# Second attention of a two-block network: heads side by side, and a fixed order of transposes, values and scores

## The chip, the core and the metric

The kernel runs on one core of a Trainium2 chip. The metric is device time in microseconds (us) for one execution of the whole program. Matrix products and transposes run on TensorE, reductions and copies on VectorE, exponentials and copies on ScalarE, element-wise work of the weights on GpSimd; SyncE issues most DMAs. Each engine works off its own instructions in the order in which the program holds them.

## What is computed

The program is a network of two blocks on a sequence of 1024 tokens of 1024 channels, in float32. The first block (gated linear attention, latent attention and an MLP, two layers) isn't touched. The second projects its input to the queries, keys and values of a dilated window attention with three groups (dilations 1, 4, 16) and eight heads of 64 channels, to the input of a Hyena convolution, and to gates. Of it the change concerns the window attention:

```python
DILATED_GROUPS = ((128, 1), (512, 4), (2048, 16))
...
    s = jnp.einsum('bdnqhe,bdnkhe->bdnhqk', qb, kw).astype(jnp.float32) * (E ** -0.5)
    s = s - slopes[:, None, None] * dist[:, None]
    s = jnp.where(valid[:, None], s, -jnp.inf)
    lse = jax.nn.logsumexp(s, axis=-1)
    p = jnp.exp(s - lse[..., None]).astype(v.dtype)
    o = jnp.einsum('bdnhqk,bdnkhe->bdnqhe', p, vw)
...
    wts = jax.nn.softmax(jnp.stack(lses, axis=0), axis=0)
    o_attn = jnp.einsum('gbsh,gbshe->bshe', wts.astype(x.dtype), jnp.stack(outs, axis=0))
```

Every query attends to the keys within a window of its group; the groups are then weighted by a softmax over their denominators.

## The kernel before

`block2` (L1540) first projects queries, keys and values, and then runs the attention in a loop over four pairs of heads (`hp`). In each turn `attention2` (L1681) loads the pair's queries, keys and values, turns the values (`vtp`, L1704) and goes through 16 steps of 128 queries: eight of part 0 (group 1, 256 keys), then eight of part 1 (groups 2 and 3 together, 256 + 128 keys). The two heads of a pair lie on partitions 0 to 63 and 64 to 127. A step is:

- **scores**: for each head one product of 256 keys (in part 1 another of 128) into a bank of its own, `as_ps` (tag "as", three buffers);
- **softmax**: for each head one VectorE operation that adds the distance bias and takes the maximum (L1737), then the negated maxima of both (`anb`, L1739), then for each head one exp on ScalarE with the sum beside it (L1741);
- **transposes**: two or three 128 x 128 blocks per head into `atp` (L1747, tag "sm", two buffers), copied to `apT` by VectorE for head 0 (L1751) and by ScalarE for head 1 (L1749);
- **values**: for each head two or three products with the values into `ao_ps` (tag "ao", one bank for four steps), copied out to `aoT` every fourth step (L1765).

A float32 product makes two records on TensorE, a transpose one. After the 16 steps `attention_weights` (L1769) weighs the two parts: the maxima and sums of part 1 go to a DRAM buffer (`abounce`, L1779) and come back in the order of part 0 (`anat`, L1780); small VectorE and ScalarE operations (L1784 to L1794) form the weights; two transposes turn them (`aw_tp`, L1798), products spread them over the heads (`aw_ps`), and VectorE and GpSimd combine the outputs.

Beside this the loop issues dense work: three column tiles of the Hyena projection per pair (`project_hyena`, L1637), each with 48 products of 512 columns (`in`, two halves of 24) and then eight transposes (`tp`, L1657) of the convolved tile `c3y`, which VectorE makes by two multiply-adds (L1208); in the last turn also gates. Their weights are split into a high and a low part by ScalarE (`w_hi`) and GpSimd or VectorE (`w_lo`, L214).

A scheduler sets the order of every engine's instructions from the order of the code, priorities, dependencies and the number of buffers of each tag. In the attention nothing else holds the order.

Of the kernel before, what the change touches and what calls it, by code (L numbers as in the profile page):

```python
# [9 lines left out]
F32 = mybir.dt.float32  # L10
# [3 lines left out]
AF = mybir.ActivationFunctionType  # L14
ALU = mybir.AluOpType
AX = mybir.AxisListType

S = 1024
# [143 lines left out]
class Kernel:  # L162
# [1474 lines left out]
    def project_hyena(self, cp, cw, ft, zd, xgd):  # L1637

        nc = self.nc
        c0 = 5120 + ft * 128  # L1640
        w = self.weights2(c0)
        u = cp.tile([128, S + 2], F32, name="c3u", tag="c3u", bufs=1)
        nc.gpsimd.memset(u[:, 0:1], 0.0)
        nc.gpsimd.memset(u[:, S + 1 : S + 2], 0.0)
        for hf in range(2):
            ps = self.project2(c0, w, hf)
            with self.tc.high_priority():
                nc.scalar.activation(u[:, 1 + hf * 512 : 513 + hf * 512], ps, AF.Identity, bias=self.bias2(c0))
        y = cp.tile([128, S], F32, name="c3y", tag="c3y", bufs=1)
        nc.scalar.activation(y, u[:, 1 : S + 1], AF.Identity, scale=cw[:, ft, 1:2], bias=cw[:, ft, 3:4])  # L1650
        self.fma(y, u[:, 0:S], cw[:, ft, 0:1], y)
        self.fma(y, u[:, 2 : S + 2], cw[:, ft, 2:3], y)
        yield
        for b in range(2):
            tp = self.PS.tile([128, 4, 128], F32, name="tp2", tag="sm", bufs=2)
# [25 lines left out]
    def attention2(self, p, hp, qkvd, yad, dist, heads):  # L1681
        nc = self.nc
        scale = 0.125
        Q, K, V = [], [], []
        for g in range(3):
            w = 1152 if g == 0 else S
            o = 64 if g == 0 else 0
            q = p.tile([128, S], F32, name="aq", tag="aq", bufs=3)
            nc.sync.dma_start(q, qkvd[hp, g, 0])
            k = p.tile([128, 1152], F32, name="ak", tag="ak", bufs=3)  # L1690
            v = p.tile([128, 1152], F32, name="av", tag="av", bufs=1)
            if g == 0:
# [23 lines left out]
        outs = []  # L1716
        for part in range(2):
            oT = p.tile([128, S], F32, name="aoT", tag="aoT", bufs=2)
            n = 256 if part == 0 else 384
            nk = n // 128  # L1720
            for i in range(8):
                ps = [self.PS.tile([128, 512], F32, name="as_ps", tag="as", bufs=3) for h in range(2)]
                qc = slice(i * 128, i * 128 + 128)
                for h in range(2):
                    r = slice(64 * h, 64 * h + 64)
                    if part == 0:
                        self.mm(ps[h][:, 0:256], Q[0][r, qc], K[0][r, i * 128 : i * 128 + 256], True, True)
                    else:
                        c0 = (i // 2) * 256
                        self.mm(ps[h][:, 0:256], Q[1][r, qc], K[1][r, c0 : c0 + 256], True, True)  # L1730
                        self.mm(ps[h][:, 256:384], Q[2][r, qc], K[2][r, qc], True, True)
                b0 = (0 if i == 0 else 512 if i == 7 else 256) if part == 0 else 768 + 384 * (i % 2)
                s = p.tile([128, 2, 384], F32, name="as", tag="as", bufs=3)
                nb = p.tile([128, 2], F32, name="anb", tag="anb", bufs=4)
                at = i if part == 0 else (i % 2) * 4 + i // 2
                for h in range(2):
                    nc.vector.tensor_tensor_reduce(s[:, h, :n], ps[h][:, :n], bt[h][:, b0 : b0 + n], scale=1.0, scalar=-3.0e38,  # L1737
                                                   op0=ALU.add, op1=ALU.max, accum_out=mst[:, part, h, at : at + 1])
                nc.vector.tensor_scalar(nb, mst[:, part, :, at], -scale, None, op0=ALU.mult)  # L1739
                for h in range(2):  # L1740
                    nc.scalar.activation(s[:, h, :n], s[:, h, :n], AF.Exp, scale=scale, bias=nb[:, h : h + 1],  # L1741
                                         accum_out=sst[:, part, h, at : at + 1])
                pt = p.tile([128, 2, 3, 128], F32, name="apT", tag="apT", bufs=2)
                for h in range(2):
                    tp = self.PS.tile([128, 4, 128], F32, name="atp", tag="sm", bufs=2)
                    for k in range(nk):
                        nc.tensor.transpose(tp[:, k], s[:, h, k * 128 : k * 128 + 128], self.ident)  # L1747
                    if h:
                        nc.scalar.activation(pt[:, h, :nk], tp[:, :nk], AF.Copy)  # L1749
                    else:  # L1750
                        nc.vector.tensor_copy(pt[:, h, :nk], tp[:, :nk])  # L1751
                if i % 4 == 0:
                    ops = self.PS.tile([128, 4, 128], F32, name="ao_ps", tag="ao", bufs=1)
                for h in range(2):
                    hc = slice(64 * h, 64 * h + 64)
                    for k in range(nk):
                        if part == 0:
                            v = V[0][:, i + k, hc]
                        elif k < 2:
                            v = V[1][:, (i // 2) * 2 + k, hc]  # L1760
                        else:
                            v = V[2][:, i, hc]
                        self.mm(ops[hc, i % 4], v, pt[:, h, k], k == 0, k == nk - 1, tile_position=(0, 64 * h))
                if i % 4 == 3:
                    nc.vector.tensor_copy(oT[:, (i // 4) * 512 : (i // 4) * 512 + 512], ops.rearrange("p a b -> p (a b)"))  # L1765
            outs.append(oT)
        return self.attention_weights(p, outs, mst, sst, yad[hp], heads)

    def attention_weights(self, p, outs, mst, sst, dst, heads):  # L1769

        nc = self.nc
        scale = 0.125
        bounce = self.DR.tile([2, 2, S], F32, name="abounce", tag="abounce", bufs=2)
        nat = p.tile([128, 2, 2, 8], F32, name="anat", tag="anat", bufs=2)
        for n, t in enumerate((mst, sst)):
            for h in range(2):
                for m in range(2):
                    to = bounce[n, h].rearrange("(w b m a) -> m w b a", b=2, m=2, a=4)[m]
# [14 lines left out]
        for part in range(2):  # L1793
            nc.vector.tensor_mul(e[:, part], e[:, part], den[:, 0])  # L1794

        tp = self.PS.tile([128, 4, 128], F32, name="aw_tp", tag="sm", bufs=2)
# [6 lines left out]
        y = outs[0]  # L1803
        for part in range(2):
            for b in range(2):
                ps = self.PS.tile([128, 4, 128], F32, name="aw_ps", tag="sm", bufs=2)
                for a in range(4):
                    self.mm(ps[:, a], heads[:, 4 * b + a], et[:, part], True, True)
                c = slice(b * 512, b * 512 + 512)
# [2 lines left out]
                else:  # L1812
                    w = p.tile([128, 512], F32, name="awt", tag="awt", bufs=1)
# [191 lines left out]
```

## Time and profile before

| what | us |
|---|---|
| median of 3 runs | 4472.46 (4463.63 to 4475.19) |
| profiled execution | 4475.41 |
| its span, first to last instruction | 4473.6 |
| TensorE busy in the span | 4130.8 (92%) |
| VectorE busy | 2082.0 (47%) |
| ScalarE busy | 1488.5 (33%) |
| GpSimd busy | 1488.1 (33%) |
| mean granted TensorE clock | 0.963 |
| the attention of the second block | from about 3395 to 3812 |

The busy shares are means over the whole program. The attention's loop takes less than a tenth of the span, so what the change does to it is read from that stretch alone. A granted clock of 1.0 is the higher of TensorE's two levels (2.4 GHz), 0.5 the lower (1.2 GHz); a value between them is a mix of both in the stretch.

### The profile page before, as it was taken

What the parts mean: (1) busy time and instruction counts of PE and PEld (TensorE: products, weight loads), DVE (VectorE), ACT (ScalarE), POOL (GpSimd) and SP (SyncE); (2) the same over time, 40 slices, a digit from 0 to 9 for tenths busy, and PEclk for the clock granted to TensorE, in tenths of its full rate; (3) what the DMA queues carried; (4) which work ended last, traced back from release to release, by engine and by line L of the source; (5) the groups of instructions that cost most, each with busy time, mean ns of one, the idle gap of its engine ahead of it and who ended that gap; (6) DMA issues with size and microseconds to landing.
All of it is one profiled execution on the core that took longest, in us unless ns stands there. A gap on an engine that the chain in (4) does not pass through costs nothing. (4 is left out here: it accounts for less than half of the span.)

```text
span 4473.6 us, 53257 instructions
## 1 busy us (share of the span) xinstructions
PE 4130.8 (92%) x20132; PEld 3220.5 (72%) x20132; DVE 2082.0 (47%) x3791; ACT 1488.5 (33%) x2822; POOL 1488.1 (33%) x1349
## 2 busy tenths in 40 slices
PE   6999888999999899888999999899999999877998
PEld 4776666888886686676888887567777676766777
DVE  6336675332335516586233324642322443577546
ACT  5435444212123515445212121323224444222222
POOL 3322455333333412254433332131230111355342
PEclk8999899999999999899999999999999999998999
DMA  6245533221111135623211111344453321645563
GB/s 195 62 134 164 166 121 92 92 61 52 47 51 58 47 106 180 202 93 116 74 44 52 43 52 48 105 123 104 113 145 83 90 86 48 188 150 157 164 193 113
DMA packets 566388, 471.21 MB, mean 105 GB/s; under 512 B 197416, under 2 KB 460670, under 8 KB 566002
## 3 DMA queue, kind: packets, MB, share of 16 engines
q1 hardware_dynamic: 375514, 367.43, 27.0%
q10 hardware_dynamic: 189880, 92.63, 7.2%
q0 software_dynamic: 736, 7.73, 0.5%
q8 instruction: 159, 2.61, 0.2%
q14 instruction: 99, 0.81, 0.1%
HBM read 364.17 MB, written 107.47 MB: 105 GB/s over the span
## 5 line engine op out<-in xcount | busy, mean ns | idle before, releaser
L214 POOL TENSOR_TENSOR w_lo<-w_raw,w_hi 128x1024 fp32r<-128x1024 f32 (+4 forms) x222 | 411.0, 1852 | 1015.8 <-ACT w_hi L208 936.4
L205 PE MATMUL dn<-act,dn_hi 128*128 128x512 f32 x2048 | 636.5, 392 | 9.8 <-ACT act L208 4.2
L662 DVE SCALAR_TENSOR_TENSOR xa<-dn,mod,xa 128x512 f32<-128x512 f32 x512 | 383.9, 750 | 277.8 <-PE dn L205 276.0
L205 PE MATMUL in<-b2h,w_hi 128*128 128x512 f32 x1152 | 467.3, 406 | 5.5 <-ACT qkv_t L1626 5.5
L205 PE MATMUL in<-b2h,w_lo 128*128 128x512 f32 x1152 | 466.6, 405 | 0.0
L205 PE MATMUL in<-b2l,w_hi 128*128 128x512 f32 x1152 | 466.3, 405 | 0.0
L208 ACT ACTIVATE w_hi<-w_raw 128x1024 fp32r<-128x1024 f32 (+4 forms) x276 | 236.8, 859 | 683.1 <-PE in L205 249.2
L205 PEld LDWEIGHTS dn<-act,dn_hi 128*128 128x128 f32 x2048 | 386.1, 189 | 95.1 <-ACT act L208 5.3
L205 PE MATMUL up<-fh,w_hi 128*128 128x512 f32 x1024 | 405.9, 396 | 0.7 <-DVE relu L632 0.4
L205 PE MATMUL up<-fl,w_hi 128*128 128x512 f32 x1024 | 402.9, 393 | 1.9 <-POOL fl L214 1.5
L205 PE MATMUL up<-fh,w_lo 128*128 128x512 f32 x1024 | 404.0, 395 | 0.0
L205 PE MATMUL dn<-act,dn_lo 128*128 128x512 f32 x1024 | 401.0, 392 | 2.8 <-POOL dn_lo L214 2.8
L632 DVE TENSOR_TENSOR relu<-up,relu 128x512 f32<-128x512 f32 x128 | 88.4, 691 | 604.5 <-ACT relu L631 604.5
L214 POOL TENSOR_TENSOR dn_lo<-dn_raw,dn_hi 128x1024 fp32r<-128x1024 f32 x64 | 151.9, 2392 | 524.5 <-ACT dn_hi L208 524.5
L205 PEld LDWEIGHTS in<-b2h,w_hi 128*128 128x128 f32 x1152 | 225.4, 196 | 57.4 <-issue 8.5
L205 PEld LDWEIGHTS in<-b2h,w_lo 128*128 128x128 f32 x1152 | 225.2, 195 | 51.6 <-issue 7.3
L205 PEld LDWEIGHTS in<-b2l,w_hi 128*128 128x128 f32 x1152 | 225.1, 195 | 50.0 <-issue 6.2
L208 ACT ACTIVATE dn_hi<-dn_raw 128x1024 fp32r<-128x1024 f32 x64 | 64.7, 1052 | 553.4 <-PE dn L205 546.1
L214 POOL TENSOR_TENSOR act<-relu,act 128x512 fp32r<-128x512 f32 x128 | 167.7, 1311 | 190.4 <-ACT act L208 190.3
L205 PEld LDWEIGHTS up<-fl,w_hi 128*128 128x128 f32 x1024 | 192.5, 188 | 49.0 <-POOL fl L214 3.2
L205 PEld LDWEIGHTS up<-fh,w_hi 128*128 128x128 f32 x1024 | 192.4, 188 | 46.6 <-issue 1.4
L205 PEld LDWEIGHTS up<-fh,w_lo 128*128 128x128 f32 x1024 | 192.6, 188 | 45.5 <-issue 1.0
(502 smaller groups left out, 8349.0 us busy)
## 6 DMA issues: line engine op xcount, KB each, us to landing
wada<-in_w_ada SPq DMA_DIRECT2D x120, 512.0 KB
w_raw<-in_w_in SPq DMA_DIRECT2D x102, 512.0 KB
w_raw<-in_w_mlp_up SPq DMA_DIRECT2D x64, 512.0 KB
dn_raw<-in_w_mlp_down SPq DMA_DIRECT2D x64, 512.0 KB
qkv<-qkv_t ACTq DMA_DIRECT2D x72, 256.0 KB
w_raw<-in_w_out SPq DMA_DIRECT2D x64, 256.0 KB
mix<-mix SPq DMA_DIRECT2D x64, 256.0 KB
spectra<-spec ACTq DMA_DIRECT2D x32, 384.0 KB
```

Of the source, the lines that this page charges most:

```text
L205: return self.nc.tensor.matmul(out, lhsT, rhs, start=start, stop=stop, **kw)
L208: self.nc.scalar.activation(hi, x, AF.Copy, **kw)
L214: return eng.tensor_sub(lo, x, hi.bitcast(F32))
L632: nc.vector.tensor_mul(sq, ps, sq)
L662: nc.vector.scalar_tensor_tensor(x[f, hf], ps, gate[:, f : f + 1], x[f, hf], op0=ALU.mult, op1=ALU.add)
```

## The change

`attention2` gets three inner functions. `scores(part, i)` makes the scores of both heads in one tile of two banks (`as_ps`, one buffer, 128 x 2 x 512), with the two heads' products of 256 keys next to each other and then those of 128, and the softmax as before. `turned` makes the transposes; in part 0 both heads' blocks go into one bank, copied out by one operation, on VectorE for even steps and on ScalarE for odd ones. `values` makes the products with the values by key block, head 1 then head 0, where before one head's blocks came after the other's. The scores of step 0 are issued first; then piece n holds the transposes of step n, the values of step n - 1 and the scores of step n + 1, and `in_order` chains the TensorE instructions of a piece one behind the other. The tag "sm" has three buffers.

```diff
-                tp = self.PS.tile([128, 4, 128], F32, name="vtp", tag="sm", bufs=2)
+                tp = self.PS.tile([128, 4, 128], F32, name="vtp", tag="sm", bufs=3)
...
+        def scores(part, i):
+
             n = 256 if part == 0 else 384
...
+            ps = self.PS.tile([128, 2, 512], F32, name="as_ps", tag="as", bufs=1)
+            qc = slice(i * 128, i * 128 + 128)
+            group = []
+            for o, w, g, c0 in ((0, 256, 0, i * 128),) if part == 0 else ((0, 256, 1, (i // 2) * 256), (256, 128, 2, i * 128)):
                 for h in range(2):
                     r = slice(64 * h, 64 * h + 64)
+                    group.append(self.mm(ps[:, h, o : o + w], Q[g][r, qc], K[g][r, c0 : c0 + w], True, True))
...
+        def turned(part, i):
+
+            nk = 2 + part
+            s = S_.pop((part, i))
+            tps = [self.PS.tile([128, 4, 128], F32, name="atp", tag="sm", bufs=3) for h in range(part + 1)]
+            to = [(tps[0][:, 2 * h : 2 * h + 2] if part == 0 else tps[h]) for h in range(2)]
+            group = [nc.tensor.transpose(to[h][:, k], s[:, h, k * 128 : k * 128 + 128], self.ident) for h in range(2) for k in range(nk)]
+            pt = P_[part, i] = p.tile([128, 2, 3, 128], F32, name="apT", tag="apT", bufs=2)
+            if part == 0:
+                both = tps[0].rearrange("p (h k) t -> p h k t", h=2)
+                if i % 2:
+                    nc.scalar.activation(pt[:, :, :2], both, AF.Copy)
+                else:
+                    nc.vector.tensor_copy(pt[:, :, :2], both)
+            else:
+                nc.vector.tensor_copy(pt[:, 0, :nk], tps[0][:, :nk])
+                nc.scalar.activation(pt[:, 1, :nk], tps[1][:, :nk], AF.Copy)
+            return group
...
+            for k in range(nk):
+                for h in (1, 0):
+                    hc = slice(64 * h, 64 * h + 64)
...
+                    group.append(self.mm(ops[hc, i % 4], v, pt[:, h, k], k == 0, k == nk - 1, tile_position=(0, 64 * h)))
...
+        steps = [(part, i) for part in range(2) for i in range(8)]
+        self.in_order(scores(*steps[0]))
+        for n in range(len(steps) + 1):
+            piece = []
+            if n < len(steps):
+                piece += turned(*steps[n])
+            if n:
+                piece += values(*steps[n - 1])
+            if n + 1 < len(steps):
+                piece += scores(*steps[n + 1])
+            self.in_order(piece)
         return self.attention_weights(p, outs, mst, sst, yad[hp], heads)
```

The order on TensorE moves at two places that matter below. The first is part 1 of a pair of heads, TensorE. Before, two steps late in that part read (`atp` are transposes of a step, `ao_ps` its values, `as_ps` scores of steps further on, one head's at a time):

```order
L1747 MATMUL atp<-ident,as 128x128 x3
L205 MATMUL as_ps<-ak,aq 128x128
L1747 MATMUL atp<-ident,as 128x128 x3
L205 MATMUL as_ps<-ak,aq 128x256
L205 MATMUL ao_ps<-apT,avt 64x128 x6
L205 MATMUL as_ps<-ak,aq 128x128
L205 MATMUL as_ps<-ak,aq 128x256
L1747 MATMUL atp<-ident,as 128x128 x6
L205 MATMUL as_ps<-ak,aq 128x128
```

In the changed program the same engine at the same place, from the last rows of dense work (`in_27171`, a half of a Hyena tile) that the pair has:

```order
L205 MATMUL in_27171<-b2l_1_21981,w_hi 128x512
L205 MATMUL in_27171<-b2h_1_21980,w_lo 128x512
L1747 MATMUL atp<-ident,as 128x128 x6
L205 MATMUL ao_ps<-apT,avt 64x128 x6
L205 MATMUL as_ps<-ak,aq 128x256 x2
L205 MATMUL as_ps<-ak,aq 128x128 x2
L1747 MATMUL atp<-ident,as 128x128 x6
L205 MATMUL ao_ps<-apT,avt 64x128 x6
```

The scores of a step stood several steps ahead of its transposes and now stand right before them; what lies between is dense work, where there is some. Nine score products stood ahead of a pair's first transposes, now those of one step.

The second place is the end of a pair, TensorE again. Before, the last values are followed by the transposes `tp` of a Hyena tile and 24 rows of dense work, of which the first are

```order
L205 MATMUL in_27099<-b2h_0_21715,w_hi 128x512
L205 MATMUL ao_ps<-apT,avt 64x128 x6
L1657 MATMUL tp_27056<-ident,c3y 128x128 x4
L1657 MATMUL tp_27064<-ident,c3y 128x128 x4
L205 MATMUL in_27099<-b2l_0_21716,w_hi 128x512
```

and the last, with the transposes of the attention weights (`aw_tp`) behind them,

```order
L205 MATMUL in_27125<-b2l_1_21975,w_hi 128x512
L205 MATMUL in_27125<-b2h_1_21974,w_lo 128x512
L205 MATMUL in_27125<-b2h_1_21976,w_hi 128x512
L1798 MATMUL aw_tp<-ident,aexp 16x128 x2
L205 MATMUL in_27125<-b2l_1_21977,w_hi 128x512
```

In the changed program the same end reads as follows (the first row holds the next pair's first scores):

```order
L205 MATMUL as_ps<-ak,aq 128x256 x2
L1747 MATMUL atp<-ident,as 128x128 x6
L205 MATMUL ao_ps<-apT,avt 64x128 x12
L1657 MATMUL tp_26992<-ident,c3y 128x128 x4
L1657 MATMUL tp_27000<-ident,c3y 128x128 x4
L1825 MATMUL aw_tp<-ident,aexp 16x128 x2
L1657 MATMUL tp_27091<-ident,c3y 128x128 x4
L1657 MATMUL tp_27099<-ident,c3y 128x128 x4
L205 MATMUL aw_ps<-aw_t,aheads 128x128 x16
L205 MATMUL in_27718<-b2h_0_21705,w_hi 128x512
```

The dense rows between the last values and `aw_tp` are gone from there; they stand ahead of the pair's earlier pieces. On VectorE one of the two multiply-adds of the next Hyena tile stands between `anat`'s product (L1817 of the changed file) and the sum behind it (L1818).

## Rows read from the trace of the kernel before

**Rows 1.** Windows: the whole attention, busy time of each engine (counts in brackets).

```profile
core 0: us, PE busy (x) PEld busy (x) DVE busy (x) ACT busy (x) POOL busy (x), PEclk, DMA share, GB/s
3395.00:3812.00 417.00, 395.69 (x2312) 287.92 (x2311) 168.59 (x478) 177.35 (x435) 52.72 (x61) 0.95 0.27 75
```

**Rows 2.** Waits of TensorE in the same stretch: total us, times, longest.

```profile
PE aw_tp L1798 <- DVE aexp L1794: 7.6, 3, 2.7
PE tp L1657 <- DVE c3y L1208: 5.2, 4, 3.6
PE as_ps L205 <- DVE amax L1737: 3.5, 3, 1.2
```

**Rows 3.** Timeline, end of the second pair: start, duration, what, count, idle before.

```profile
3561.77 0.18 ACT L1741 ACTIVATION_READ_ACCUMULATOR as<-as,anb 128x1 f32 x1
...
3572.26 0.18 DVE L1790 TENSOR_TENSOR aden<-aexp,anat 128x16 f32<-128x16 f32 x1 [3.08 <-DMA anat<-abounce]
...
3573.29 0.38 PE L1798 MATMUL aw_tp<-ident,aexp 128*16 128x128 f32 x2 [2.26 <-DVE aexp L1794]
...
3573.74 0.40 PE L205 MATMUL in<-b2h,w_lo 128*128 128x512 f32 x1
...
3573.97 0.39 PE L205 MATMUL in<-b2h,w_hi 128*128 128x512 f32 x1
```

**Rows 4.** Timeline of TensorE, part 0 of the first pair.

```profile
3420.84 0.70 PE L205 MATMUL as_ps<-ak,aq 64*128 64x256 f32 x2
3421.47 0.67 PE L205 MATMUL ao_ps<-apT,avt 128*64 128x128 f32 x8
3422.06 0.66 PE L1747 MATMUL atp<-ident,as 128*128 128x128 f32 x4
3422.65 0.70 PE L205 MATMUL as_ps<-ak,aq 64*128 64x256 f32 x4
3423.28 0.66 PE L205 MATMUL ao_ps<-apT,avt 128*64 128x128 f32 x8
```

**Rows 5.** Timeline, one step of part 1 of the first pair.

```profile
3441.74 0.90 PE L1747 MATMUL atp<-ident,as 128*128 128x128 f32 x6
...
3442.57 0.70 PE L205 MATMUL as_ps<-ak,aq 64*128 64x128 f32 x4
...
3443.09 0.56 DVE L1737 CUSTOM_DVE_ANT_0 as<-as_ps,abias 128x384 f32<-128x384 f32 x1
...
3443.20 1.15 PE L205 MATMUL ao_ps<-apT,avt 128*64 128x128 f32 x12
...
3443.69 0.17 DVE L1739 TENSOR_SCALAR anb<-amax 128x2 f32<-128x2 f32 x1
...
3444.51 0.60 ACT L1741 ACTIVATE as<-as,anb 128x384 f32<-128x384 f32 x1
...
3444.91 0.89 PE L1747 MATMUL atp<-ident,as 128*128 128x128 f32 x6
```

**Rows 6.** Timeline of TensorE, first transposes and end of the second pair's steps.

```profile
3518.04 0.44 PE L1747 MATMUL atp<-ident,as 128*128 128x128 f32 x2
...
3564.48 1.09 PE L1657 MATMUL tp<-ident,c3y 128*128 128x128 f32 x8
```

**Rows 7.** Timeline, an exp of head 0 and the transposes that waited for it.

```profile
3430.40 0.61 ACT L1741 ACTIVATE as<-as,anb 128x384 f32<-128x384 f32 x1 [0.78 <-DVE anb L1739]
...
3431.16 0.33 PE L1747 MATMUL atp<-ident,as 128*128 128x128 f32 x1 [0.16 <-ACT as L1741]
```

**Rows 8.** Timeline of VectorE: a long `anb`, and a multiply-add of a Hyena tile.

```profile
3498.20 1.62 DVE L1739 TENSOR_SCALAR anb<-amax 128x2 f32<-128x2 f32 x1
...
3502.04 1.27 DVE L1208 SCALAR_TENSOR_TENSOR c3y<-c3u,conv_w,c3y 128x1024 f32<-128x1024 f32 x1
```

**Rows 9.** Windows: two stretches elsewhere with a half-idle TensorE (columns as in rows 1).

```profile
670.00:680.00 10.00, 6.09 (x22) 3.82 (x22) 5.29 (x7) 5.98 (x11) 6.68 (x6) 1.00 0.78 247
3840.00:3850.00 10.00, 5.13 (x17) 4.46 (x18) 8.86 (x13) 0.75 (x2) 7.07 (x6) 0.54 0.68 226
```

**Rows 10.** Timeline of TensorE, scores in a stretch at the lower clock.

```profile
3704.80 1.22 PE L205 MATMUL as_ps<-ak,aq 64*128 64x256 f32 x2
```

More of the change, by code (lines that the diff above doesn't have):

```diff
@@ L1654, in project_hyena @@
         for b in range(2):
-            tp = self.PS.tile([128, 4, 128], F32, name="tp2", tag="sm", bufs=2)
+            tp = self.PS.tile([128, 4, 128], F32, name="tp2", tag="sm", bufs=3)
             for a in range(4):
@@ L1715, in attention2 @@
         sst = p.tile([128, 2, 2, 8], F32, name="asum", tag="asum", bufs=2)
-        outs = []
-        for part in range(2):
-            oT = p.tile([128, S], F32, name="aoT", tag="aoT", bufs=2)
+        outs, S_, P_, O_ = [], {}, {}, {}
+        def scores(part, i):
             n = 256 if part == 0 else 384
[L1720 to L1723, printed above, removed]
+            ps = self.PS.tile([128, 2, 512], F32, name="as_ps", tag="as", bufs=1)
+            qc = slice(i * 128, i * 128 + 128)
+            group = []
+            for o, w, g, c0 in ((0, 256, 0, i * 128),) if part == 0 else ((0, 256, 1, (i // 2) * 256), (256, 128, 2, i * 128)):
@@ L1724, in attention2 @@
                 for h in range(2):
                     r = slice(64 * h, 64 * h + 64)
+                    group.append(self.mm(ps[:, h, o : o + w], Q[g][r, qc], K[g][r, c0 : c0 + w], True, True))
+            b0 = (0 if i == 0 else 512 if i == 7 else 256) if part == 0 else 768 + 384 * (i % 2)
+            s = S_[part, i] = p.tile([128, 2, 384], F32, name="as", tag="as", bufs=3)
+            nb = p.tile([128, 2], F32, name="anb", tag="anb", bufs=4)
+            at = i if part == 0 else (i % 2) * 4 + i // 2
@@ new lines, in scores @@
+            for h in range(2):
+                nc.vector.tensor_tensor_reduce(s[:, h, :n], ps[:, h, :n], bt[h][:, b0 : b0 + n], scale=1.0, scalar=-3.0e38,
+                                               op0=ALU.add, op1=ALU.max, accum_out=mst[:, part, h, at : at + 1])
+            nc.vector.tensor_scalar(nb, mst[:, part, :, at], -scale, None, op0=ALU.mult)
+            for h in range(2):
+                nc.scalar.activation(s[:, h, :n], s[:, h, :n], AF.Exp, scale=scale, bias=nb[:, h : h + 1],
+                                     accum_out=sst[:, part, h, at : at + 1])
@@ new lines, in scores @@
+            return group
[15 more added lines that the diff above has]
+                nc.scalar.activation(pt[:, 1, :nk], tps[1][:, :nk], AF.Copy)
+            return group
@@ L1726, in attention2, with values @@
+        def values(part, i):
+            nk = 2 + part
+            pt = P_.pop((part, i))
+            if i == 0:
+                outs.append(p.tile([128, S], F32, name="aoT", tag="aoT", bufs=2))
+            if i % 4 == 0:
+                O_[0] = self.PS.tile([128, 4, 128], F32, name="ao_ps", tag="ao", bufs=1)
+            ops, group = O_[0], []
+            for k in range(nk):
+                for h in (1, 0):
+                    hc = slice(64 * h, 64 * h + 64)
                     if part == 0:
-                        self.mm(ps[h][:, 0:256], Q[0][r, qc], K[0][r, i * 128 : i * 128 + 256], True, True)
-                    else:
-                        c0 = (i // 2) * 256
-                        self.mm(ps[h][:, 0:256], Q[1][r, qc], K[1][r, c0 : c0 + 256], True, True)
-                        self.mm(ps[h][:, 256:384], Q[2][r, qc], K[2][r, qc], True, True)
@@ L1732, in attention2 @@
[L1732 to L1763, printed above, removed]
@@ L1764, in attention2 @@
-                if i % 4 == 3:
-                    nc.vector.tensor_copy(oT[:, (i // 4) * 512 : (i // 4) * 512 + 512], ops.rearrange("p a b -> p (a b)"))
-            outs.append(oT)
+                        v = V[0][:, i + k, hc]
+                    elif k < 2:
+                        v = V[1][:, (i // 2) * 2 + k, hc]
+                    else:
+                        v = V[2][:, i, hc]
+                    group.append(self.mm(ops[hc, i % 4], v, pt[:, h, k], k == 0, k == nk - 1, tile_position=(0, 64 * h)))
@@ new lines, in values @@
+            if i % 4 == 3:
+                nc.vector.tensor_copy(outs[part][:, (i // 4) * 512 : (i // 4) * 512 + 512], ops.rearrange("p a b -> p (a b)"))
+            return group
+        steps = [(part, i) for part in range(2) for i in range(8)]
[9 more added lines that the diff above has]
+            self.in_order(piece)
@@ L1794, in attention_weights @@
             nc.vector.tensor_mul(e[:, part], e[:, part], den[:, 0])
-        tp = self.PS.tile([128, 4, 128], F32, name="aw_tp", tag="sm", bufs=2)
+        tp = self.PS.tile([128, 4, 128], F32, name="aw_tp", tag="sm", bufs=3)
         for part in range(2):
@@ L1805, in attention_weights @@
             for b in range(2):
-                ps = self.PS.tile([128, 4, 128], F32, name="aw_ps", tag="sm", bufs=2)
+                ps = self.PS.tile([128, 4, 128], F32, name="aw_ps", tag="sm", bufs=3)
                 for a in range(4):
```

## The prediction

> **What bounds the kernel now.** The change touches the second attention, four pairs of heads at 3395 to 3812 us of the span, so I read that stretch, first the busy time of each engine. TensorE works 395.7 of the 417 us there, VectorE 168 and ScalarE 177 [rows 1]: TensorE is the bound, and the stage gets shorter only if it has less to do or waits less. The list of its waits comes next. What is left of the 417, some 21 us, goes mostly to three places: the transposes of the attention weights (`aw_tp`, L1798) 7.6, those of the hyena projections (`tp`, L1657) 5.2, the scores for a bank still being reduced 3.5 [rows 2], 16.3 together. Last I read the timeline of a step in either part, to see what one step costs and how long its softmax takes from scores to transposes. Beside the steps TensorE has the dense projections (`in`): 0.23 us from one to the next [rows 3].
>
> **The order.** All that follows rests on where the dense matmuls stand. In the changed program the pieces are fixed, and the scheduler puts eight to ten dense matmuls ahead of each piece until the pair's 144 are used up. Counted over the four pairs, 22 of the 64 pieces have no cover or only three dense matmuls: n = 12 to 15 of the first pair, 10 to 15 of the others. Nor does a dense matmul stand between a pair's last values and `aw_tp`, where before 24 stood in the second pair. (Before, too, steps without dense matmuls occur, but there the scores run four and a half steps ahead.)
>
> **1. Work taken from TensorE.** In part 0 one step is now transposes 0.59, scores 0.63, values 0.59 [rows 4] (each from its start to the next row's). The scores show what side by side is worth: two records, one head, take 0.63 (from 3420.84), and four records, both heads, the same 0.63 (from 3422.65). Eight value records take 0.59, no more than four transposes, so they too run beside each other. A part-0 step, 1.81, stays what it is. In part 1 a step repeats after 3441.74 to 3444.91 = 3.17: transposes 0.83, scores 0.63 for one head (3442.57 to 3443.20) and 0.63 for the other, and the rest, 1.08, values [rows 5]. Changed: values 0.59 and for the third key block 0.22 (two more transposes are worth 0.83 - 0.59 = 0.24, two matmuls side by side with two records each about the same), 0.81; scores 0.63 and 0.21 for a pair half as wide, 0.84; with the transposes 2.48, that is 0.69 less. A pair of heads then takes 8 x 1.81 + 8 x 2.48 = 34.3, and some 1.9 at the ends and beside dense matmuls: 36.2. Before, the second pair ran from 3518.04 to 3564.48, 46.4 [rows 6]; 12 dense matmuls lie in it (2.8), 0.2 is waiting, and nine score matmuls came before it, at 0.31 (paired) to 0.63 each, taken as 4: 47.5. That is 11.3 saved in each of three pairs. The first pair runs side by side already in part 0: 5.4 to 7.5. Sum **-41**, bounds -22 (if part 1 keeps its pace in the first pair and gains half in the others) and -45.
>
> One rule speaks for more. The rows show that part 0 had its side-by-side gain before, and that transposes (0.59 and 0.83 a step) don't take part. The Trainium skill, TensorEngine Tiling (Array Packing), Overview, Theoretical Speedup, gives up to twice the speed where a dimension is 64 or less; by it the scores and values, 36 of the 47.5 us of a pair, would halve, -72 in place of -41. It is the last rival below.
>
> **2. The wait of an uncovered piece.** Piece n is T(n), V(n - 1), S(n + 1), so between S(n) and T(n) stands nothing but dense work, and the softmax of step n lies open. From the rows of part 1 [rows 5]: scores until the first reduce can start, 0.84 (one head's 3442.57 to 3443.09 is 0.52, here the group of four comes first); a reduce 0.56; second reduce to `anb` 0.60; `anb` to the second exp 0.82; a head's exp to its transposes 0.76 [rows 7]. Sum 3.58. With ten dense matmuls the cover is 2.3 + 0.84 + 0.41 (the first head's transposes, half of 0.83) = 3.55: no stall. Without them the step is 3.58 + 0.41 + 0.81 = 4.80 against 2.48 of work: 2.3 idle. Eighteen at 2.3; three last pieces, where the next pair's first scores (0.63) stand ahead, at 1.7; one with three dense matmuls at 1.65. Sum **+48**. Lower bound: the head's own exp could release its three transposes and the chain be 0.6 shorter, +35; upper: VectorE's copy of the transposes gets ahead of a reduce, +0.56 each, +60.
>
> **3. The attention weights.** After a pair's last exp the maxima and sums go to HBM and back. From the last accumulator read at 3561.77 to the product that needs them at 3572.26 are 10.5, to `aw_tp` at 3573.29 11.5; the dense matmuls hid all but 2.26 of it [rows 3]. Now two 1.27 us products of the hyena projection [rows 8] stand in VectorE's row there, one of them behind that product: +1.3. TensorE has left the last transposes, two steps of values and eight `tp`, about 3.0. So 12.8 - 3.0 = 9.8 idle where the transfer is as slow as here; I take 9.5 four times, **+38** (bounds 28, without the product and with a transfer 1.2 faster, and 48, with one 2.5 slower). Waiting behind it on TensorE are `aw_ps` and the next pair's dense work. `tp` itself now comes right behind the values with its input perhaps unready: **+3** (0 to 5.2). The three old waits go: **-16**.
>
> **4. Work of other stages inside the chain.** A chain without slack is hit by what the scheduler puts between. `anb`, normally 0.17, took 1.62 while GpSimd subtracted weights; a product of the projection on VectorE takes 1.27 [rows 8]. Three such hits per pair at about 1 us: **+12** (0 to 29, twice per projection and pair).
>
> **5. The clock.** A half-idle TensorE may lose its clock. At 670 to 680 it was busy 6.1 of 10 us and had full clock; at 3840 to 3850 busy 5.1, granted 0.54, the lower of its two levels most of the time [rows 9]. There an uncovered piece has 2.5 of 4.8 busy. At the lower level a pair of scores took 1.22 where it takes 0.70 at the higher [rows 4, 10]; 0.75 more of the 2.06 us of a piece that stand on its path (0.41, 0.81, 0.84) and some latency is 1.75, times 22 = 38 if all are hit. The first pieces of each stretch follow full work, so I take a third: **+13**.
>
> **The sum.** -41 + 48 + 38 + 3 - 16 + 12 + 13 = +57 us. The profiled execution took 4475.4, so 4532; that run lies 3 above the median of the runs shown: **4529 us**. Other parts: one more `sm` buffer and the joint copy of both heads in part 0 cost nothing visible, since VectorE and ScalarE are at 40%.
>
> **Rivals.**
> - **TensorE's work decides** (faster). If transposes find their exps ready, only the saved work shows: 4475 - 41 - 16 = 4418 and a few us of waits, 4423. It decides from where the new waits of 2 to 5 (114 by my sum) stay under 57. For it: that the covered pieces have room, and that VectorE and ScalarE are idle more than half of the time [rows 1]. Against: 22 pieces and four ends with nothing to issue.
> - **Half of the waits** (about 4484). The chain of an uncovered piece shorter by 0.9 (20 us), no hits (12), full clock (13): +12. For it: with the old run-ahead gone, each engine has only one step to serve.
> - **The clock falls in every uncovered piece**: 25 more, 4554. For it: the row at 3840; against: the row at 670. The Trainium skill, TensorE: Matmul & The Clock Gate, Part 1: The HAM clock gate, says that the rate follows how busy TensorE has been of late; both rows bear that out, and by it this rival gains weight where idle time is spread over a whole stretch.
> - **Scores and values at twice the speed**: by the rows that would need scores and values at half their time in part 0 too, where pairs of heads took 0.63 and 0.59 [rows 4]; 31 more saved, 4498. The rule of the page under part 1 gives this time; the trace does not bear it out.
>
> **How the numbers follow.** A measurement can tell about 0.3%, 4459 to 4486. My forecast, 4505 to 4555, gets 0.52, the clock 0.15 (to 4580), twice the speed 0.05, half of the waits 0.17 (4459 to 4505, of which 0.10 within 0.3%), TensorE's work alone 0.11. Slower 0.52 + 0.15 + 0.05 + 0.07 = 0.79, same 0.10, faster 0.11. The range 4470 to 4575 leaves out the faster case, the lowest 0.03 of half of the waits and the upper 0.05 of the clock.
>
> **What would show it.** Right: `atp` waiting for ScalarE's exp about 2.3 us in some 20 pieces of the profile after, `aw_tp` waiting four times about 9.5, part 1 pieces with 2.5 us of work, covered pieces with no idle time. Wrong: `atp` waits under 1 us (chain too long in my sum), `aw_tp` under 5 (a faster way through HBM), values at 1.08 (no overlap), a granted clock near 0.5 in the uncovered stretches (the clock rival).

## The result, and the profile after

The changed kernel takes 4534.74 us (median of 4 runs, 4529.19 to 4541.57), the kernel before 4469.45 us (4 runs, 4463.63 to 4475.19). The ratio is 1.0147 with a 95% interval of 1.0126 to 1.0167: slower by 65 us. The profiled execution has a span of 4539.8 us, 66.2 above before's.

The loss lies in the stretch that the change touches. A measure of it that recurs below is the time from the first transposes of the attention (`atp`) to the first product of the phase behind it (`dft_ps` with the matrix `dftm`). Before, it ran from 3414.7 to 3842.3, 427.6 us. After, the views of the two tiles (engine, operation, durations in ns, first and last start) say:

```profile
L1747 PE MATMUL atp<-ident,as x320: 270/273/477, 3415.0 to 3836.8; 128*128 128x128 f32 x160
L205 PEld LDWEIGHTS dft_ps<-pr_hi,dftm x256: 186/192/338, 3903.8 to 4257.3; 128*128 128x128 f32 x128
```

That is 488.8 us, **61 more**. TensorE's busy time is the same in both stretches (windows, columns as in [rows 1]; before, then after), so all of the 61 is idle time, 84.0 us in place of 22.4, and the work that was saved has been lost again to slower work:

```profile
3414.70:3842.30 427.60, 405.21 (x2352) 296.71 (x2353) 172.93 (x471) 175.17 (x421) 55.59 (x62) 0.95 0.29 82
3415.00:3903.80 488.80, 404.79 (x2360) 308.73 (x2358) 171.71 (x465) 176.56 (x413) 59.33 (x63) 0.83 0.25 72
```

What TensorE waits for there answers to [rows 2] (total us, times, longest):

```profile
PE atp L1747 <- ACT as L1737: 43.8, 27, 2.1
PE aw_tp L1825 <- DVE aexp L1821: 29.5, 4, 8.8
PE as_ps L205 <- issue: 3.9, 3, 1.3
```

The transposes of a step now wait for its exps, the transposes of the attention weights wait four times, and the old waits for `c3y` are gone. The scores wait at three ends of pairs, where the view names no releaser. One piece without dense work, in the second pair (timeline, answers to [rows 5]):

```profile
3579.68 1.65 PE L205 MATMUL as_ps<-ak,aq 64*128 64x256 f32 x8
3581.37 0.56 DVE L1733 CUSTOM_DVE_ANT_0 as<-as_ps,abias 128x384 f32<-128x384 f32 x1 [2.73 <-PE as_ps L205]
...
3582.45 0.17 DVE L1735 TENSOR_SCALAR anb<-amax 128x2 f32<-128x2 f32 x1
3582.66 0.61 ACT L1737 ACTIVATE as<-as,anb 128x384 f32<-128x384 f32 x1 [3.49 <-DVE anb L1735]
...
3583.42 1.54 PE L1747 MATMUL atp<-ident,as 128*128 128x128 f32 x6 [2.09 <-ACT as L1737]
```

The eight score records of both heads stand first, then nothing: reduce, `anb`, exp, and 2.09 us after TensorE's last score the first transposes start. The timeline has 18 such waits of 2.09 us. The scores take 1.65 us here; in a covered piece, at 3558.15 with a granted clock of 1.00, the same eight records took 0.92. The windows show the second pair's covered pieces, its uncovered ones, and the stretch behind its wait for `aw_tp`:

```profile
3516.00:3566.00 50.00, 49.57 (x297) 36.84 (x296) 16.69 (x54) 21.84 (x54) 5.30 (x8) 1.00 0.29 93
3566.00:3610.00 44.00, 31.66 (x200) 23.02 (x199) 14.41 (x44) 14.16 (x41) 5.26 (x3) 0.61 0.11 25
3616.00:3630.00 14.00, 13.97 (x53) 12.29 (x54) 5.74 (x6) 3.34 (x6) 3.61 (x4) 0.50 0.22 68
```

With cover TensorE has no idle time to speak of and the higher clock all through. Without cover it is busy 72% of the time, mostly at the lower level, and behind the wait for the weights it stays there for 14 us in which TensorE doesn't pause.

What TensorE's work itself takes is in the groups by line (count, busy us, mean ns, idle before; groups overlap, so that their busy times don't add up to TensorE's). Before, the scores, values and transposes were busy for 84.1, 66.8 and 56.7 us, and `aw_ps` for 17.2. After:

```profile
L1747 PE MATMUL atp<-ident,as 128*128 128x128 f32 x320 | 64.7, 315 | 44.5 <-ACT as L1737 43.8
L205 PE MATMUL as_ps<-ak,aq 64*128 64x256 f32 (+1 forms) x384 | 62.3, 438 | 3.9 <-issue 3.9
L205 PE MATMUL ao_ps<-apT,avt 128*64 128x128 f32 x640 | 62.0, 340 | 0.0
L205 PE MATMUL aw_ps<-aw_t,aheads 16*128 16x128 f32 x128 | 28.8, 421 | 0.0
```

189.0 in place of 207.6 for the first three: less work, but slower work. The mean of a transpose is 315 ns; at the higher level it is 284, as the runs below show.

### The profile page after: what moved, and what is told of

Its sections match the earlier page's. It is cut to its first block, busy times and chain, and to the rows that moved or that the text cites. A ratio compares the mean times of both kernels' runs of the same rounds, so it can differ in the third digit from the quotient of the medians.

```text
span 4539.8 us, 53207 instructions
## 1 busy us (share of the span) xinstructions
PE 4125.7 (91%) x20132; PEld 3232.5 (71%) x20132; DVE 2079.3 (46%) x3775; ACT 1488.4 (33%) x2806; POOL 1491.2 (33%) x1349
```

## The experiments

All times of before are those of runs on the same chip. The theory: the saved work is real, and is more than eaten up by a softmax that lies open in pieces without dense work, by the uncovered wait for the weights, and by the lower clock that follows both. Rivals: the one two-bank buffer of the scores costs the time; or heads side by side save nothing.

**Scores two steps ahead.**

```diff
         self.in_order(scores(*steps[0]))
+        self.in_order(scores(*steps[1]))
         for n in range(len(steps) + 1):
...
+            if n + 2 < len(steps):
+                piece += scores(*steps[n + 2])
             if n:
                 piece += values(*steps[n - 1])
-            if n + 1 < len(steps):
-                piece += scores(*steps[n + 1])
```

> The scores of step n + 2 in piece n, between the transposes of step n and the values of step n - 1, instead of the scores of step n + 1 at the end. My theory (the loss is that a step's softmax lies open between its scores and its transposes, and that the dense work is used up as cover before the attention weights): atp waits for exps fall from 43.8 us to under 5, the dense work returns between the last values and aw_tp (19 to 31 products stand there now), its wait falls from 29.5 to about 10, the mean clock rises to 0.96, and the saved work shows: 4435 us, 4425 to 4450. Rival 1 (one two-bank buffer for the scores is what costs): the scores wait for the reduces instead, about 1 to 1.5 us in each late piece, 25 to 40 us in all, 4470 or more. Rival 2 (heads side by side save nothing): waits gone, but the time stays at before's, 4469.

The scores also move ahead of the values within a piece. 4434.42 us, ratio to before 0.9909 (0.9885 to 0.9933): **faster than both kernels**, by 42 us than before (4476.55 on that chip), by about 100 than the changed one. TensorE's longest wait in the attention, and three groups by line:

```profile
PE aw_tp L1826 <- DVE aexp L1822: 9.5, 3, 3.6
```

```profile
L205 PE MATMUL as_ps<-ak,aq 64*128 64x256 f32 (+1 forms) x384 | 52.0, 376 | 0.0
L1747 PE MATMUL atp<-ident,as 128*128 128x128 f32 x320 | 51.6, 284 | 0.2
L205 PE MATMUL ao_ps<-apT,avt 128*64 128x128 f32 x640 | 48.4, 283 | 0.0
```

No wait for exps or for the scores' bank is left, though the buffer is the same single one: the first rival falls. The work is 152.0 us against 207.6 before: the second falls. The attention takes 377.7 us, 50 less than before. All three parts of the theory go at once here, so this run doesn't divide the loss among them. A late piece of the second pair, without dense work, now reads:

```profile
3535.74 0.88 PE L1747 MATMUL atp<-ident,as 128*128 128x128 f32 x6
3536.55 0.92 PE L205 MATMUL as_ps<-ak,aq 64*128 64x256 f32 x8
3537.40 0.88 PE L205 MATMUL ao_ps<-apT,avt 128*64 128x128 f32 x12
3538.21 0.88 PE L1747 MATMUL atp<-ident,as 128*128 128x128 f32 x6
```

0.81 + 0.85 + 0.81 = 2.47 us from transposes to transposes, against the 2.48 of the prediction's first step and 3.17 before [rows 5]. Since the pieces need little cover now, the scheduler leaves 17 to 31 dense products between a pair's last values and `aw_tp`.

**Values alternating between the heads, alone, in the kernel before.**

```diff
-                for h in range(2):
-                    hc = slice(64 * h, 64 * h + 64)
-                    for k in range(nk):
+                group = []
+                for k in range(nk):
+                    for h in (1, 0):
+                        hc = slice(64 * h, 64 * h + 64)
...
+                self.in_order(group)
```

> The kernel before with one edit: the value products of a step by key block, head 1 then head 0, held in that order; all else as before. My theory: a pair of products with 64 columns each runs side by side, values take 46 to 50 us of TensorE in place of 61.7, and the time falls by 12 to 15 us to about 4455. Rival 2 (side by side saves nothing here, since TensorE busy in the attention is 394 us after and 396 before): 61 us as before and 4469.

4463.66 us against 4476.55, ratio 0.9970 (0.9955 to 0.9984): 13 us faster.

```profile
L205 PE MATMUL ao_ps<-apT,avt 128*64 128x128 f32 x640 | 50.4, 283 | 0.3 <-ACT apT L1749 0.2
```

66.8 us before, 50.4 now: most of the 16 us taken from TensorE show in the time, since nothing new waits.

**Idle products in the uncovered pieces of the changed kernel.**

```diff
                 piece += scores(*steps[n + 1])
+                if n + 1 >= (13 if hp == 0 else 10):
+                    x = self.H[0, 0][0]
+                    idle = self.PS.tile([128, 512], F32, name="idle_ps", tag="sm", bufs=3)
+                    for a in range(8):
+                        piece.append(self.mm(idle, x[:, 0:128], x, a == 0, a == 7))
             self.in_order(piece)
```

> The changed kernel with eight products of 512 columns, whose result nobody reads, behind the scores of each piece that has no dense cover (n from 10, in the first pair from 13). They take 1.84 us where 2.09 us are waited, so they cost nothing by themselves. My theory (the lower clock in the uncovered stretches costs some 20 us on top of the waits): the granted clock stays at 1.0 in these stretches, atp waits fall to about 0.2 each, and the time falls by 10 to 25 us to 4510 to 4525. Rival (the lower clock falls into the waits and costs nothing): 4535, with the clock up all the same. If the products get in the way of the transposes' bank: 4545.

4514.69 us, ratio 1.0087 (1.0064 to 1.0110), below the changed kernel's 1.0147 (1.0126 to 1.0167): 168 products that do nothing make it 20 us faster by the medians, 27 by the ratios, each to before on its own chip.

```profile
PE aw_tp L1830 <- DVE aexp L1826: 37.3, 4, 9.8
PE atp L1747 <- ACT as L1737: 4.7, 9, 1.6
```

```profile
L1747 PE MATMUL atp<-ident,as 128*128 128x128 f32 x320 | 59.0, 284 | 6.6 <-ACT as L1737 4.7
L205 PE MATMUL as_ps<-ak,aq 64*128 64x256 f32 (+1 forms) x384 | 54.1, 376 | 0.0
L205 PE MATMUL ao_ps<-apT,avt 128*64 128x128 f32 x640 | 48.4, 283 | 0.0
```

The window of the second pair's uncovered pieces, with a clock of 0.92 where the changed kernel had 0.61:

```profile
3566.00:3610.00 44.00, 34.00 (x250) 23.86 (x250) 18.29 (x55) 17.16 (x44) 5.44 (x5) 0.92 0.29 72
```

The three groups need 161.5 us here and 189.0 in the changed kernel: 27.5 us were the lower clock. And the wait for the weights grows from 29.5 to 37.3, as TensorE gets there sooner.

**The attention weights moved into the next pair.** The attention gets the generator of the pair before and runs its two parts ahead of pieces 3 and 4; the output tile is taken at step 3, when it is first written.

```diff
-                rest = self.attention2(p, hp, qkvd, yad, dist, heads)
+                rest = self.attention2(p, hp, qkvd, yad, dist, heads, rest if hp else None)
                 next(rest)
...
-                    next(rest, None)
+            for _ in rest:
+                pass
...
-            if i == 0:
+            if i == 3:
                 outs.append(p.tile([128, S], F32, name="aoT", tag="aoT", bufs=2))
...
         for n in range(len(steps) + 1):
+            if late and n in (3, 4):
+                next(late, None)
```

> The changed kernel with the attention weights of a pair worked out inside the next pair's pieces (aw_tp ahead of piece 3, aw_ps ahead of piece 4), and after the loop for the last pair. My theory: the four waits of aw_tp, 29.5 us, go, the lower clock behind them too, 25 to 40 us off, 4495 to 4510; the 22 uncovered pieces stay (atp 40 to 44 us). Rival (the transfer through HBM takes its time anyway, and something else waits): less than 10 us off, 4525 or more, with the copy of the values or the next transposes waiting instead.

4522.68 us, ratio 1.0107 (1.0073 to 1.0141), whose interval overlaps the changed kernel's. My numbers were missed. The wait left `aw_tp` and came back at the second of the two tiles' `tp`, which had stood right behind it:

```profile
PE tp L1658 <- DVE aden L1821: 25.1, 4, 7.7
```

The timeline of the second pair's end, and below it one row of the third's, say why:

```profile
3602.52 1.45 PE L1658 MATMUL tp<-ident,c3y 128*128 128x128 f32 x8
...
3605.17 1.24 ACT L1651 ACTIVATE c3y<-c3u,conv_w 128x1024 f32<-128x1024 f32 x1 [0.52 <-ACT xg_t L1660]
...
3606.45 1.28 DVE L1208 SCALAR_TENSOR_TENSOR c3y<-c3u,conv_w,c3y 128x1024 f32<-128x1024 f32 x1 [1.07 <-ACT c3y L1651]
...
3607.74 0.17 DVE L1820 TENSOR_TENSOR aden<-aexp,anat 128x16 f32<-128x16 f32 x1
3607.82 1.28 DVE L1208 SCALAR_TENSOR_TENSOR c3y<-c3u,conv_w,c3y 128x1024 f32<-128x1024 f32 x1
...
3609.24 1.09 PE L1658 MATMUL tp<-ident,c3y 128*128 128x128 f32 x4 [5.27 <-DVE aden L1821]
...
3722.87 0.18 DVE L1820 TENSOR_TENSOR aden<-aexp,anat 128x16 f32<-128x16 f32 x1 [2.31 <-DMA anat<-abounce]
```

The two `tp` follow the last values directly, and `c3y` has one buffer. So the second tile's `c3y` can begin only when the first `tp` has read it, and then come ScalarE's part (L1651) and VectorE's two multiply-adds: 6.7 us from `tp` to `tp`, in 5.3 of which TensorE has nothing to do. In the second and fourth pair (waits of 5.27 and 5.15) that is all; the operations on the data from HBM (`aden` on `anat`), which VectorE's row still holds between the multiply-adds, take 0.17 and wait for nothing. In the first and third (7.04 and 7.68) VectorE waits there for the data, for 1.65 and 2.31 us. Of the 25.1 some 4 are therefore the trip through HBM; the rest is a chain of the Hyena tiles that the wait for the weights had hidden.

**The changed kernel in the scheduler's own order**: `self.in_order(piece)` and the chain of the first scores left out, all else kept.

> The changed kernel without the chains between the TensorE instructions of a piece: the functions and tiles of the change, the scheduler's own order. Its order has one or two steps' scores ahead, one to six dense products in nearly every step up to the last, and 21 to 34 between the last values and aw_tp. My theory (where the dense work and the scores stand decides): atp waits under 8 us, aw_tp under 12, side by side kept in part, since score and value products of the two heads often stand apart: 4440 to 4460. Rival (the one two-bank buffer for scores is what costs): scores or transposes wait 25 us or more, 4480 or more.

4460.50 us against 4473.61, ratio 0.9968 (0.9952 to 0.9983).

```profile
PE aw_tp L1824 <- DVE aexp L1820: 7.9, 3, 4.7
PE atp L1747 <- ACT as L1737: 1.3, 4, 0.8
```

```profile
L205 PE MATMUL as_ps<-ak,aq 64*128 64x256 f32 (+1 forms) x384 | 78.2, 392 | 0.0
```

The waits are gone with the single buffer in place, which disposes of that rival again. But the scheduler tears the two heads' scores apart: 78.2 us, near the 84.1 of before. The attention takes 419.9 us, 42 more than with pieces in order and scores two ahead. A fixed order is worth having; the one of the change has the scores in the wrong place.

**Heads one after the other, in the order with scores two ahead.**

```diff
-            for o, w, g, c0 in ((0, 256, 0, i * 128),) if part == 0 else ((0, 256, 1, (i // 2) * 256), (256, 128, 2, i * 128)):
-                for h in range(2):
-                    r = slice(64 * h, 64 * h + 64)
+            for h in range(2):
+                r = slice(64 * h, 64 * h + 64)
+                for o, w, g, c0 in ((0, 256, 0, i * 128),) if part == 0 else ((0, 256, 1, (i // 2) * 256), (256, 128, 2, i * 128)):
...
-            for k in range(nk):
-                for h in (1, 0):
-                    hc = slice(64 * h, 64 * h + 64)
+            for h in range(2):
+                hc = slice(64 * h, 64 * h + 64)
+                for k in range(nk):
```

> The kernel with scores two steps ahead, but in each step all of head 0's score products before head 1's, and all of head 0's value products before head 1's; order of the pieces kept. My theory: scores of the two heads then share the engine only at their seams, TensorE needs 20 to 30 us more (as_ps 55 to 62 in place of 47.6, ao_ps about 58 in place of 44.5), 4454 to 4464. Rival (the fixed order gives the gain, not the pairs): 4434 as with pairs.

4441.31 us, ratio 0.9922 (0.9897 to 0.9947): the same as with alternating heads (0.9885 to 0.9933) within the intervals. Attention 383.1 us, 5 more.

```profile
L205 PE MATMUL ao_ps<-apT,avt 128*64 128x128 f32 x640 | 55.9, 282 | 0.0
L205 PE MATMUL as_ps<-ak,aq 64*128 64x256 f32 (+1 forms) x384 | 52.3, 376 | 0.0
```

My 20 to 30 us were too much. The values lose 7.5 us when they don't alternate; the scores lose nothing, as long as the two heads' products stand next to each other. So the gain on the scores comes from adjacency, not from alternation; before, many stood one head at a time among other work.

**Both: scores two ahead, and the weights in the next pair.**

> Scores two steps ahead, and the attention weights of a pair worked out inside the next pair's pieces. In the run with the weights moved alone, the wait had come back at tp (25.1 us): VectorE's row held the product that waits for HBM ahead of the multiply-add of a Hyena tile. Here 51 dense products (11.7 us) stand between the last values and the second tile's tp, so my theory is that this wait is covered: aw_tp 9.5 us gone, tp as before, 4422 to 4432. Rival (a row of VectorE blocked for 10 us stops something whatever TensorE does): tp or atp wait 8 us or more, 4434 or more.

4405.35 us, ratio **0.9840 (0.9819 to 0.9862)**, the fastest of all, 68 us below before and 17 below the lowest that I had expected.

```profile
PE tp L1658 <- DVE c3y L1208: 7.6, 8, 3.1
```

`aw_tp` doesn't wait any more, and `tp` waits 7.6 instead of 25.1: dense products, 51 between the two tiles' `tp` at a pair's end, now fill the chain of the second tile. The attention takes 364.4 us, 13.3 less than with scores two ahead alone: 6.4 less idle time, and 6.9 less busy time (350.1 in place of 357.0) at a granted clock of 0.97 in place of 0.95. The medians lie 29 us apart, the two profiled executions 27.2; of these, 8.7 lie ahead of the attention and 5.2 behind it, where the two programs have the same code. Those I can't account for.

**More idle products, ahead of the wait for the weights.** 32 behind the eight, first between the last values and the first `tp`:

```diff
+        idle = self.PS.tile([128, 512], F32, name="idle2_ps", tag="sm", bufs=3)
+        last = [self.mm(idle, x[:, 0:128], x, a == 0, a == 31) for a in range(32)]
+        self.in_order(piece[-1:] + last)
         return self.attention_weights(p, outs, mst, sst, yad[hp], heads, last[-1:])
```

> The changed kernel with the eight idle products per uncovered piece and 32 more (7.3 us) between a pair's last values and aw_tp, which waited 37.3 us in all in the run with the eight alone. They fill time that was waited, so what goes is the lower clock behind that wait (17 to 20 us at 0.5 after each pair there). My theory: 15 to 25 us off the run with eight, 4490 to 4500, no stretch over 7 us at the lower clock in the attention, aw_tp waits 5 to 10. Rival (the clock behind the waits costs little, as aw_ps waits for copies anyway): 4510 to 4515.

4525.74 us, 1.0111 (1.0086 to 1.0135), and this wait:

```profile
PE tp L1657 <- DVE c3y L1208: 21.5, 4, 5.5
```

The products stood ahead of `tp`; `tp` frees the one buffer of `c3y`, so the next tile's multiply-adds and its `tp` came later. That tells nothing of the clock. Then the same 32 between `tp` and `aw_tp`:

```diff
+        last = [self.last_tp] + [self.mm(idle, x[:, 0:128], x, a == 0, a == 31) for a in range(32)]
         for part in range(2):
-            nc.tensor.transpose(tp[:16, part], e[:, part].rearrange("p h i -> p (h i)"), self.ident)
+            last.append(nc.tensor.transpose(tp[:16, part], e[:, part].rearrange("p h i -> p (h i)"), self.ident))
+        self.in_order(last)
```

> The 32 idle products again, now between the first tp of a pair's end and aw_tp, where TensorE waited 37.3 us in four waits with eight idle products per uncovered piece alone; ahead of tp, as in the run before, they had held up tp, the tile c3y that it frees and with it the next tp (21.5 us). VectorE's row is now the one of the run with eight alone. They take 7.3 of 9.3 us waited at each place. My theory: the clock stays at the higher level behind the wait, where 17 to 20 us at the lower level stood at each pair's end; aw_tp waits 6 to 10 us in all, aw_ps busy 17 to 20 us in place of 28.8, and 12 to 25 us go, 4490 to 4503. Rival (the lower level there costs little, since what follows waits for copies anyway): 4510 to 4518. Second rival (the clock falls at the transposes and narrow products behind the wait, whatever stood before them): aw_ps stays at 28 us.

4513.12 us, 1.0093 (1.0064 to 1.0122): no gain over the eight alone.

```profile
PE atp L1747 <- ACT as L1737: 8.8, 9, 2.0
PE aw_tp L1833 <- DVE aexp L1826: 7.6, 4, 2.0
```

```profile
L205 PE MATMUL aw_ps<-aw_t,aheads 16*128 16x128 f32 x128 | 22.4, 351 | 0.0
```

The wait is filled and `aw_ps` is down from 28.8 to 22.4, but not to 17: the clock still falls, later, in the row of `aw_ps` (granted 0.69 from 3615 to 3620 us, 0.50 from 3620 to 3622). Part of the gain is eaten by the exps' waits (4.7 before, 8.8 here). What the lower clock behind the wait for the weights costs in the end stays open; that it costs in the uncovered pieces is shown by the run with eight.

## Why the prediction was right

The forecast was 4529, 60 above the median of before; it came out at 4535. Step by step, for the attention, in us:

| step | forecast | measured |
|---|---|---|
| 1. work taken from TensorE | -41 | -46 (207.6 to 161.5, at the higher clock, idle products) |
| 2. uncovered pieces | +48 | +45.5 (41.6 in 22 pieces, and 3.9 for the scores' bank) |
| 3. attention weights | +38 | +29.5 (37.3 at the higher clock) |
| `tp` | +3 | 0 |
| old waits | -16 | -16 |
| 4. work of other stages in the chain | +12 | at most 2 (the rest of the 43.8 of `atp`, in five covered pieces) |
| wait for loaded values (`vtp`) | none | +0.5 (0.7, 0.2 before) |
| 5. clock | +13 | about 43 (27.5 in the steps, 11.6 in `aw_ps`, 3.9 in `tp`, busy 17.7 and before 13.8) |
| sum | +57 | +58.5 of the 61 seen |

Another 3 of the 61 come from scores that stood ahead of the first transposes before: 80.4 of their 84.1 us lie in the measured stretch, after the change 61.6 of 62.3.

**Step 2 held to the piece.** The count from the order of the changed program gave 18 pieces at 2.3; the trace has 18 at 2.09. The piece with three dense products waited 1.57 (1.65 forecast), and the three last pieces of pairs 2.3, 1.8 and 2.3 (1.7 forecast), each in two parts. The 1.31 ahead of the next pair's first scores, in each of them, is the bank of the score buffer, which the step didn't have: at the third pair's end the second reduce is done at 3716.95 and these scores start at 3717.16. The covered pieces waited at most 0.5: eight to ten dense products are just enough.

**Step 3 had the chain's length right and the rest of TensorE's work too small.** In the timeline of the third pair's end, from the last exp's accumulator to `aw_tp`:

```profile
3719.21 0.19 ACT L1737 ACTIVATION_READ_ACCUMULATOR as<-as,anb 128x1 f32 x1
...
3720.32 2.44 PE L205 MATMUL ao_ps<-apT,avt 128*64 128x128 f32 x24
...
3722.70 1.09 PE L1657 MATMUL tp<-ident,c3y 128*128 128x128 f32 x8
...
3730.15 0.18 DVE L1817 TENSOR_TENSOR aden<-aexp,anat 128x16 f32<-128x16 f32 x1 [2.19 <-DMA anat<-abounce]
3730.24 1.28 DVE L1208 SCALAR_TENSOR_TENSOR c3y<-c3u,conv_w,c3y 128x1024 f32<-128x1024 f32 x1
...
3732.25 0.58 PE L1825 MATMUL aw_tp<-ident,aexp 128*16 128x128 f32 x2 [8.46 <-DVE aexp L1821]
```

3719.21 to 3732.25 is 13.0 us (12.8 forecast), the multiply-add of 1.28 in it as seen in the order. But TensorE was busy 4.6 us of it, not 3.0, in part at the lower clock. The four ends took 13.4, 11.3, 13.0 and 12.3 us, and TensorE waited 8.8, 5.9, 8.5 and 6.4 of them. In the second and fourth the data from HBM were there before VectorE came to the product that needs them, and what came last were the Hyena tile's two multiply-adds, which had first waited for ScalarE's part of `c3y`: a path that the step didn't have, and the one that came back when the weights were moved.

**Steps 4 and 5 were mis-sized, in opposite directions.** What the lower clock adds to one piece was right, 1.75 forecast. The windows of one piece of the first pair and one of the second, from transposes to transposes, differ by 1.80:

```profile
3474.37:3479.26 4.89, 2.75 (x26) 1.94 (x26) 1.77 (x6) 1.79 (x6) 0.00 (x0) 1.00 0.01 2
3583.42:3590.11 6.69, 4.60 (x26) 3.37 (x27) 2.46 (x7) 1.79 (x6) 0.00 (x0) 0.50 0.00 0
```

The share of such pieces was wrong. Step 5 took a third, from two rows that disagreed [rows 9]; granted was 0.89, 0.61, 0.75 and 0.70 over the uncovered pieces of the four pairs, so the lower level held for more than half of their time. And it reached beyond them, into `aw_ps` and `tp`, which the step didn't have at all. The clock rival, at 25 more, was nearly right on the term, and its sign, a clock near 0.5 in the uncovered stretches, was nearly met. Step 4 put three hits on each pair where the covered pieces show next to none. That the errors cancel is luck: steps 1 to 4 and `tp` came out 29 below the forecast in sum, step 5 came out 30 above it. With only step 4 or only step 5 mended the forecast would have been 4519 or 4559, both in the range.

Of the rivals, TensorE's work alone did not decide, because its condition (steps 2 to 5 under 57) was missed: 45.5 + 29.5 + 2 + 43 = 120 (114 by the sum). The run with scores two ahead is what that rival describes: with the new waits gone, 4434, against 4423 worked out for it. The rule of the Trainium skill (TensorEngine Tiling (Array Packing), Overview, Theoretical Speedup), up to twice the speed where a dimension is 64 or less, would, by an estimate from that figure, have taken scores and values from 150.9 to 75.5 us; they came to 102.5 (idle products) and 100.4 (scores two ahead), a factor of 1.5, with part of them side by side already before [rows 4]. The trace agrees with the direction and stays below the limit that the page names.

## What to carry to other kernels

When an order is fixed by hand, write down what stands between an operand's producer and its consumer in the piece that has no filler work left, and compare it with the length of the chain through the other engines; here one more step of distance, at no cost in buffers of the scores, turned 1.5% slower into 0.9% faster. Filler work that covers one wait is missing at the next one: follow it to where it used to stand. And before a wait is moved away, look at what stands behind it: here the next transposes hung on a chain of their own, through one buffer, and when the weights' wait of 29.5 us was moved, 25.1 came back under another name, until dense work stood in the gap.

## What the runs showed of the hardware

- The lower clock stayed on when the wait was over. Behind the second pair's wait of 5.9 us for the weights it lasted for 14 us without a pause of TensorE (busy 13.97 of 14.00, granted 0.50), while ten transposes, 32 records of products with 16 rows and ten dense products ran. With all but 1.9 us of that wait filled by idle products, it fell in the row of the products with 16 rows (granted 0.69, then 0.50).
- Work that nobody reads can pay: eight products of 512 columns in each uncovered piece brought the granted clock there from 0.61 to 0.92 and the time down by about 20 us.
- Products of two heads on different 64 rows overlapped in these runs when they stood next to each other (52.3 us head by head, 52.0 alternating); products on different 64 columns gained from alternation (55.9 and 48.4).
